# A short-convolution layer on one core: the scale's half of each later adaLN piece loaded from Pool's queue

## The chip, the core and the metric

The kernel runs on one core of a Trainium2 chip. The metric is the device time of one execution in microseconds (us). Before the change it is 904.07 us, the median of three runs (903.63 to 904.27). A profiled execution of the same kernel, whose trace is read below, took 904.01 us, of which 902.2 us are the span that the trace covers.

## The reference

With one layer, 256 tokens, a model width of 2048 and a branch width of 4096, the reference comes down to this (all in float32):

```
h = rmsnorm(x, norm_g)                              # x: 256 x 2048
mod = silu(c) @ ada_w + ada_b                       # ada_w: 2048 x 6144
shift, scale, gate = split(mod, 3)                  # 2048 each
h = h * (1 + scale) + shift
b, c_, v, g = split(h @ sc_w_in, 4)                 # sc_w_in: 2048 x 16384
u = causal_depthwise_conv(c_ * v, sc_conv_w)        # width 3
y = b * u * silu(g)
out = rmsnorm(x + gate * (y @ sc_w_out), final_g)   # sc_w_out: 4096 x 2048
```

The columns of `ada_w` lie in three blocks of 2048: those of the shift, of the scale and of the gate. No product with `sc_w_in` can be made for a row block k (128 rows of the 2048) before shift and scale of that block are known.

## The kernel before, in words

**Start.** SP issues the loads of x (four of 512 KB, L218), then the columns of `ada_w` for the first two row blocks k = 0 and 1, for shift and scale (twelve loads, 4 MB, L231), then the first weights, `raw0` (two of 256 KB, L198). VectorE (DVE) sums the columns weighted by silu(c) (L413, L415), TensorE adds them up, ScalarE (ACT) writes the high part of the modulated tokens into `hT` (L328), and Pool the low part of k = 1 (L433). All of this is pinned in the order in which it is written (`in_order`), engine by engine.

**First half of the input projection (`mm_s`).** Float32 products are made as three products of a high and a low part: a load of weights (`raw_s`, L538) is split by ACT (`hi`, L354) and DVE (`lo`, L359), and TensorE multiplies `hi` with both parts of the tokens and `lo` with the high part (L495). A function `plan()` writes down a list of steps, 16 groups of four column blocks, each taken over those row blocks that are ready by the plan's own costs, so that the groups are opened with k = 0 and 1 and finished later. What has been summed so far is kept in `acc` by ACT (L516) or DVE (L518), and put back by ACT (L528).

**adaLN behind the first group.** Between those steps the plan places 56 steps `ada`: seven groups of two row blocks, in eight pieces each. A piece (`ada_piece`) takes one of four tiles `at` (128 x 1024 floats, `bufs=4`) and fills it with two DMAs of 256 KB, one with the columns of the shift, one with those of the scale (L464), both on SP's queue. DVE adds the two halves together, with one instruction for each of the two rows in the tile (L476 for the first row of a group, L478 for all others), each over 512 columns of which 256 belong to either half. So every such instruction needs both loads. After the last piece of a group TensorE turns the sums (L485), DVE reduces them (L486), and the tokens of two more row blocks become ready (L324 to L335).

**Order on the queues.** Beyond the pinned start, the tile framework arranges each engine's queue when the kernel is built. It goes by a priority, which is the order in the program unless `later` moves it, and by which instructions have their buffers and inputs in its own model of the time. A load that needs a tile comes up for its queue when the tile's last users are done in that model. The weights have three places of 1 MB, cut in half for loads of 512 KB.

**Rest.** The second half of the input projection (`mm_b`) runs with all row blocks ready, the gate's columns are loaded into the same four tiles (`at_g`, L612) and summed over the partitions by Pool with small DMAs on its own queue (L625 and L626, their sum in L627), and then comes the output projection (L731).

Of the kernel before, what the change touches and what calls it, by code (L numbers as in the profile page):

```python
# [13 lines left out]
P = 128  # L14
# [103 lines left out]
def short_conv_layer(ctx: ExitStack, tc: tile.TileContext, x, c, norm_g, ada_w, ada_b, w_in, conv_w, w_out, final_g, out):  # L118
    nc = tc.nc
# [68 lines left out]
    @contextmanager  # L188
    def later(n):

        now = tc.cur_priority
        tc.cur_priority = now + n
        yield
        tc.cur_priority = now
# [29 lines left out]
    adas = ada_w[0].rearrange("(k p) (s f) -> p k s f", p=P, s=3)  # L224
# [229 lines left out]
    def ada_piece(k0, nk, piece):  # L454
        w = nk * P
        kk = ASLOT // (2 * w)
        if piece == 0:
            sums[k0] = adap.tile([P, 2, 2 * P], F32, tag="gv", name="gv")
        gv = sums[k0][:, :, 0:w]
        j = piece * kk  # L460
        at = adap.tile([P, ASLOT], F32, tag="at", name="at", bufs=4)
        at4 = at.rearrange("p (k s f) -> p k s f", k=kk, s=2)
        for s in range(2):
            nc.sync.dma_start(at4[:, :, s, :], adas[:, j : j + kk, s, k0 * P : k0 * P + w])  # L464
        with later(GIVE):
            ada_sums(j, kk, at4, gv)
        if j + kk == KT:
            with later(-LEAD):
                ada_done(k0, nk, gv)

    def ada_sums(j, kk, at4, gv):
        for i in range(kk):
            c_k = silu_c[:, j + i : j + i + 1]
            if j + i == 0:
                with behind(ended):
                    nc.vector.tensor_scalar_mul(gv, at4[:, i], c_k)  # L476
            else:
                nc.vector.scalar_tensor_tensor(out=gv, in0=at4[:, i], scalar=c_k, in1=gv, op0=ALU.mult, op1=ALU.add)  # L478

    def ada_done(k0, nk, gv):  # L480

        tp = psum.tile([P, 4, P], F32, tag="sm", name="tp_g", bufs=2)
        gs = const.tile([P, 4], F32, tag="gs", name="gs", bufs=2)
        for o in range(2 * nk):
            nc.tensor.transpose(tp[:, o, :], gv[:, o // nk, (o % nk) * P : (o % nk + 1) * P], ident)  # L485
        nc.vector.reduce_sum(gs[:, 0 : 2 * nk], tp[:, 0 : 2 * nk, :], axis=mybir.AxisListType.X)  # L486
        modulate(k0, nk, gs[:, 0 : 2 * nk])
# [80 lines left out]
    for kind, *step in plan():  # L568
        if kind == "ada":
            ada_piece(*step)  # L570
        else:
            ch, k1 = step[0], step[3]
            part(*step)
            if step[2] == 0 and len(acc) in LATER:
                with tc.issue_after(last_mm[0].ins), behind(ended):
                    if len(acc) == LATER[0]:
                        rows2 = rows_tile("rows2")
                        nc.sync.dma_start(rows2[:, :], conv_w.rearrange("w (k p) -> (w k) p", p=P))
                    else:
                        turn(rows2, 0, 96, cw)  # L580
            whole[ch] += k1 == KT
            if k1 == KT and whole[ch] == 4:
                mixed(ch)
# [354 lines left out]
```

## Time and profile before

| what | before |
|---|---|
| time, median of three | 904.07 us |
| profiled execution: its time, its span | 904.01 us, 902.2 us |
| TensorE busy | 887.1 us, 98% of the span |
| DVE, ACT, Pool busy | 676.2, 484.5, 88.0 us |
| first product with `sc_w_in` starts | 24.86 us |
| `mm_s` ends, `mm_b` ends | 378.56 us, 726.72 us |
| loads on the changed line (L464) | 112 of 256 KB, issued from 21.2 to 208.6 us |

Times within the trace are counted from the start of its span. In the rows of a timeline the columns are start, duration, engine, line, operation, what it writes and reads, and, in brackets, the idle time of the engine ahead of it and what ended that. SPq and POOLq are the sequencers that issue DMAs. In the table by stretches each engine's busy time is followed by the granted clock of TensorE, the mean busy share of the 16 DMA engines (it can be a little over 1, as packets overlap) and the GB/s that they moved.

### The profile page before, as it was taken

What the parts mean: (1) busy time and instruction counts of PE and PEld (TensorE: products, weight loads), DVE (VectorE), ACT (ScalarE), POOL (GpSimd) and SP (SyncE); (2) the same over time, 40 slices, a digit from 0 to 9 for tenths busy, and PEclk for the clock granted to TensorE, in tenths of its full rate; (3) what the DMA queues carried; (4) which work ended last, traced back from release to release, by engine and by line L of the source; (5) the groups of instructions that cost most, each with busy time, mean ns of one, the idle gap of its engine ahead of it and who ended that gap; (6) DMA issues with size and microseconds to landing.
All of it is one profiled execution on the core that took longest, in us unless ns stands there. A gap on an engine that the chain in (4) does not pass through costs nothing.

```text
span 902.2 us, 16405 instructions
## 1 busy us (share of the span) xinstructions
PE 887.1 (98%) x6997; PEld 850.1 (94%) x6997; DVE 676.2 (75%) x665; ACT 484.5 (54%) x429; POOL 88.0 (10%) x95
## 2 busy tenths in 40 slices
PE   7999999999999999999999999999999999999996
PEld 4899999999999999999999999999999988888885
DVE  5889989888888866765966677565555578879896
ACT  6767866665548766644433434444434445444443
POOL 0000000000000034024224203420000000000000
PEclk9999999999999999999999999999999999999999
DMA  9999999999998587688887788776666476674662
GB/s 309 367 369 369 362 313 353 351 370 354 350 328 289 162 277 245 194 257 243 282 242 241 249 283 259 232 221 199 198 188 188 141 288 224 191 275 132 197 231 94
DMA packets 159595, 235.01 MB, mean 260 GB/s; under 512 B 6805, under 2 KB 105285, under 8 KB 159137
## 3 DMA queue, kind: packets, MB, share of 16 engines
q1 hardware_dynamic: 156384, 226.56, 76.9%
q0 software_dynamic: 3008, 7.34, 2.9%
q8 instruction: 55, 0.90, 0.4%
q14 instruction: 20, 0.16, 0.0%
q10 hardware_dynamic: 128, 0.04, 0.0%
HBM read 224.49 MB, written 2.10 MB: 251 GB/s over the span
## 4 chain that ended last, share of the span: by engine, by line
PE 92%; DMA 4%; ACT 1%; SPq 1%; DVE 1%; issue 1%; ACTq 0%
PE mm_b L495 39%; PE mm_s L495 36%; PE mm_w L731 7%; PE mm_o L731 6%; PE mm L731 4%; DMA at<-in_ada_w_dram 2%; DMA raw_s<-in_sc_w_in_dram 1%; SPq L231 1%; ACT hi L354 1%; DMA raw_o<-in_sc_w_out_dram 1%; DMA x<-in_x_dram 1%; PE tp_g L485 0%; ACT mm_s L528 0%; ACT acc L516 0%; DVE lo L762 0%
## 5 line engine op out<-in xcount | busy, mean ns | idle before, releaser
L495 PE MATMUL mm_s<-hT,hi 128*128 128x256 f32 x2048 | 350.2, 277 | 1.7 <-ACT hT L328 1.0
L495 PE MATMUL mm_b<-hT,hi 128*128 128x256 f32 x2048 | 348.2, 276 | 0.0
L495 PEld LDWEIGHTS mm_s<-hT,hi 128*128 128x128 f32 x2048 | 308.4, 188 | 2.3 <-ACT hT L328 1.2
L495 PEld LDWEIGHTS mm_b<-hT,hi 128*128 128x128 f32 x2048 | 308.4, 188 | 0.0
L495 PE MATMUL mm_b<-hT,lo 128*128 128x256 f32 x1024 | 282.7, 276 | 0.0
L495 PE MATMUL mm_s<-hT,lo 128*128 128x256 f32 x1024 | 282.0, 277 | 0.1
L359 DVE TENSOR_TENSOR lo<-raw,hi 128x2048 fp32r<-128x2048 f32 (+1 forms) x66 | 151.9, 2302 | 99.6 <-ACT hi L354 99.4
L354 ACT CAST hi<-raw 128x2048 fp32r<-128x2048 f32 (+1 forms) x66 | 123.7, 1874 | 191.3 <-PE mm_b L495 152.4
L495 PEld LDWEIGHTS mm_b<-hT,lo 128*128 128x128 f32 x1024 | 192.3, 188 | 0.0
L495 PEld LDWEIGHTS mm_s<-hT,lo 128*128 128x128 f32 x1024 | 191.7, 188 | 0.3 <-DVE lo L359 0.3
L359 DVE TENSOR_TENSOR lo<-raw_s,hi 128x2048 fp32r<-128x2048 f32 (+1 forms) x80 | 149.8, 1877 | 40.5 <-ACT hi L354 39.9
L354 ACT CAST hi<-raw_s 128x2048 fp32r<-128x2048 f32 (+1 forms) x80 | 124.0, 1557 | 57.2 <-PE mm_s L495 51.2
L478 DVE SCALAR_TENSOR_TENSOR gv<-at,silu_c,gv 128x512 f32<-128x512 f32 x105 | 78.7, 749 | 3.6 <-DMA at<-in_ada_w_dram 1.9
L516 ACT COPY acc<-mm_s 128x1024 f32<-128x1024 f32 x54 | 54.7, 1014 | 42.1 <-PE mm_s L495 42.0
L359 DVE TENSOR_TENSOR lo<-raw_o,hi 128x2048 fp32r<-128x2048 f32 x22 | 50.4, 2291 | 23.4 <-ACT hi L354 23.4
L354 ACT CAST hi<-raw_o 128x2048 fp32r<-128x2048 f32 x22 | 42.0, 1908 | 46.2 <-PE mm_w L731 12.0
L627 POOL TENSOR_TENSOR gacc<-gacc,z 128x512 f32<-128x512 f32 x28 | 48.3, 1726 | 109.0 <-DMA z<-gacc 109.0
L731 PE MATMUL mm_w<-hi,y 128*128 128x512 f32 x184 | 58.8, 389 | 0.0
L731 PE MATMUL mm_o<-hi,y 128*128 128x512 f32 x176 | 55.3, 389 | 0.0
L621 DVE SCALAR_TENSOR_TENSOR gacc<-at_g,silu_c,gacc 128x512 f32<-128x512 f32 x60 | 46.9, 782 | 6.0 <-DMA at_g<-in_ada_w_dram 4.8
L625 POOL DMA_DIRECT2D z<-gacc x28 | 15.7, 560 | 348.7 <-DVE acc L562 284.7
L731 PEld LDWEIGHTS mm_w<-hi,y 128*128 128x128 f32 x184 | 34.5, 188 | 7.1
(153 smaller groups left out, 685.9 us busy)
## 6 DMA issues: line engine op xcount, KB each, us to landing
raw<-in_sc_w_in_dram SPq DMA_DIRECT2D x64, 1024.0 KB, 5.9
raw_s<-in_sc_w_in_dram SPq DMA_DIRECT2D x47, 1024.0 KB, 7.8
raw_o<-in_sc_w_out_dram SPq DMA_DIRECT2D x32, 1024.0 KB, 5.2
at<-in_ada_w_dram SPq DMA_DIRECT2D x114, 256.0 KB, 8.0
raw_s<-in_sc_w_in_dram SPq DMA_DIRECT2D x33, 512.0 KB, 7.1
at_g<-in_ada_w_dram SPq DMA_DIRECT2D x32, 512.0 KB, 7.9
at<-in_ada_w_dram SPq DMA_DIRECT2D x6, 512.0 KB, 9.4
x<-in_x_dram SPq DMA_DIRECT2D x4, 512.0 KB, 6.2
```

Of the source, the lines that this page charges most:

```text
L231: nc.sync.dma_start(at[:, :, s, :], adas[:, j : j + kk, s, 0 : NK0 * P])
L354: nc.scalar.copy(hi[:, :n], raw[:, :n])
L359: last_low[0] = nc.vector.tensor_tensor(out=lo[:, :n], in0=raw[:, :n], in1=hi[:, :n].bitcast(F32), op=ALU.subtract)
L478: nc.vector.scalar_tensor_tensor(out=gv, in0=at4[:, i], scalar=c_k, in1=gv, op0=ALU.mult, op1=ALU.add)
L495: mm = last_mm[0] = nc.tensor.matmul(dst, w, h[k], start=begins and left, stop=ends, skip_group_check=True)
L516: nc.scalar.copy(acc[ch, q], bank)
L621: nc.vector.scalar_tensor_tensor(out=ga, in0=at3[:, i, :], scalar=s, in1=ga, op0=ALU.mult, op1=ALU.add)
L625: nc.gpsimd.dma_start(turned[0 : P - away], ga[away:P])
L627: nc.gpsimd.tensor_tensor(out=ga, in0=ga, in1=turned, op=ALU.add)
L731: nc.tensor.matmul(dst, y[a], b, start=opens and i == 0, stop=ends and i == 2, skip_group_check=True)
```

## The change

Of the two DMAs of each of the 56 pieces the one with the shift's columns (s = 0) stays on SP's queue and the one with the scale's (s = 1) goes to Pool's. The tiles, the bytes, and the instructions that read them are the same.

```diff
@@ -461,7 +461,8 @@
         at = adap.tile([P, ASLOT], F32, tag="at", name="at", bufs=4)
         at4 = at.rearrange("p (k s f) -> p k s f", k=kk, s=2)
         for s in range(2):
-            nc.sync.dma_start(at4[:, :, s, :], adas[:, j : j + kk, s, k0 * P : k0 * P + w])
+            queue = (nc.sync, nc.gpsimd)[s]
+            queue.dma_start(at4[:, :, s, :], adas[:, j : j + kk, s, k0 * P : k0 * P + w])
         with later(GIVE):
             ada_sums(j, kk, at4, gv)
         if j + kk == KT:
```

The loads of the first group (L231), the weights and the gate's columns stay on SP's queue.

## The prediction, made before the changed kernel was run

> **What bounds the kernel now.** I read the page first, then the waits of TensorE in the stage that the change touches, then the table by stretches, then the chain that ended last and the timeline around the start.
>
> ```profile
> PE 887.1 (98%) x6997; PEld 850.1 (94%) x6997; DVE 676.2 (75%) x665; ACT 484.5 (54%) x429; POOL 88.0 (10%) x95
> PE mm_s L495 <- ACT hT L328: 1.0, 1, 1.0
> PE mm_s L495 <- ACT hi L354: 0.6, 1, 0.6
> ```
>
> The first row says that TensorE hardly rests. The other two are all of its waits between 24 and 110 us; from 110 to 400 us the same view shows none. So once the products with the weights have begun, at most 1.6 us can be won in the stage of the change, and each microsecond by which that beginning moves moves the end. When it begins is the first thing to look at.
>
> ```profile
> 0.00:1.00 1.00, 0.00 (x0) 0.00 (x0) 0.09 (x2) 0.00 (x0) 0.41 (x5) 1.00 0.00 0
> 1.00:2.00 1.00, 0.00 (x0) 0.00 (x0) 0.00 (x0) 0.00 (x0) 0.29 (x1) 1.00 0.32 57
> 2.00:3.00 1.00, 0.00 (x0) 0.00 (x0) 0.00 (x0) 0.87 (x1) 0.00 (x0) 1.00 0.79 143
> 3.00:4.00 1.00, 0.00 (x0) 0.00 (x0) 0.00 (x0) 0.41 (x1) 0.00 (x0) 1.00 0.85 295
> 10.00:12.00 2.00, 2.00 (x6) 0.92 (x5) 1.71 (x7) 0.03 (x1) 0.00 (x0) 1.00 1.10 363
> 18.00:20.00 2.00, 1.74 (x16) 1.74 (x17) 1.93 (x3) 2.00 (x7) 0.00 (x0) 1.00 1.10 347
> 50.00:80.00 30.00, 30.00 (x267) 30.00 (x266) 27.46 (x33) 21.18 (x20) 0.00 (x0) 1.00 1.07 370
> ```
>
> In each row the last two figures are the DMA engines' busy share and their GB/s. They are full from about 4 us on, and still full at 50 to 80 us. TensorE and DMA are both at their limit here, and DVE is at 27.46 of 30 us. These rows from the timelines of DVE, ACT and TensorE show what the start waits for:
>
> ```profile
> 13.21 0.49 DVE L413 TENSOR_SCALAR gv<-at,silu_c 128x512 f32<-128x512 f32 x1 [0.74 <-DMA at<-in_ada_w_dram]
> 16.32 6.78 DVE L415 SCALAR_TENSOR_TENSOR gv<-at,silu_c,gv 128x512 f32<-128x512 f32 x9 [0.26 <-DMA at<-in_ada_w_dram]
> 22.97 1.33 ACT L354 CAST hi<-raw 128x512 fp32r<-128x512 f32 x2 [1.84 <-DMA raw<-in_sc_w_in_dram]
> 24.86 0.74 PE L495 MATMUL mm_s<-hT,hi 128*128 128x256 f32 x4 [0.99 <-ACT hT L328]
> ```
>
> DVE starts its sums when the first columns land and is then busy without a break but for 0.26 us; ACT waits 1.84 us for `raw0`, the last load of the start. Both ways to the first product at 24.86 us begin with a DMA that waits its turn in a full queue. What lands ahead of `raw0` delays the first product.
>
> **What the change removes.** 56 issues of 256 KB each leave SP's queue (two loads of that size belong to the first group and stay).
>
> ```profile
> at<-in_ada_w_dram SPq DMA_DIRECT2D x114, 256.0 KB, 8.0
> L464 SPq DMA_DIRECT2D at<-in_ada_w_dram x112: 367/460/2052, 21.2 to 208.6; - x112
> DMA to landing us min/median/max: 4.1/8.0/9.7
> SPq L464 <- DVE gv L478: 19.5, 32, 2.2
> SPq L538 <- DVE lo L359: 146.9, 56, 8.4
> ```
>
> At a median of 0.460 us this frees 56 x 0.46 = 26 us of SP. It is worth nothing on the path: SP waits 146.9 us for weight places that DVE gives back, and 19.5 us for `at` tiles, and the half that stays on SP waits for the same tile. Without this cover the gain could be no more than the 1.6 us that TensorE waits. The bytes are unchanged: 8.0 us from issue to landing is a backlog of some 3 MB at 370 GB/s, mostly turn-taking.
>
> **What it adds to Pool.** 56 issues, on a queue whose loads the trace shows only for the gate. The first two rows are one of Pool's two issuing lines (count, then minimum, median, maximum in ns) and its time from issue to landing in us; the others are all that Pool does before 311 us, but for four constants in its first half microsecond.
>
> ```profile
> L625 POOL DMA_DIRECT2D z<-gacc x28: 532/557/698, 311.6 to 593.1; - x28
> DMA to landing us min/median/max: 2.4/3.9/8.4
> 0.74 0.20 POOL masks.py:197 MEMSET ident<- 128x128 f32 x1 [0.29 <-POOLq L925]
> 1.01 0.29 POOL masks.py:199 TENSOR_SCALAR_AFFINE_SELECT ident<-ident 128x128 f32<-128x128 f32 x1
> 26.02 0.91 POOL L433 TENSOR_TENSOR hT<-xs,hT 128x256 fp32r<-128x256 f32 x1 [24.71 <-ACT xs L429]
> ```
>
> 56 x 0.56 = 31 us of Pool, in time in which it is idle: nothing on the path. From issue to landing I expect 2.4 to 9.7 us, the ends of Pool's and of SP's rows, and take Pool's median of 3.9, since the new loads stand in no backlog of their own queue. That wins nothing either, as every sum on L478 needs the shift's half as well.
>
> **What it moves.** The order on a queue is not that of the program:
>
> ```profile
> 21.15 0.99 SPq L464 DMA_DIRECT2D at<-in_ada_w_dram  x2
> 22.19 0.47 SPq L538 DMA_DIRECT2D raw_s<-in_sc_w_in_dram  x1
> 22.70 0.98 SPq L464 DMA_DIRECT2D at<-in_ada_w_dram  x2
> 23.72 0.58 SPq L538 DMA_DIRECT2D raw_s<-in_sc_w_in_dram  x1
> 24.91 3.76 SPq L464 DMA_DIRECT2D at<-in_ada_w_dram  x4
> 30.09 0.35 SPq L578 DMA_DIRECT2D rows<-in_sc_conv_w_dram  x1
> 30.83 3.18 SPq L538 DMA_DIRECT2D raw_s<-in_sc_w_in_dram  x4
> ```
>
> In the program L578 stands behind the tenth column group, with nine loads of `raw_s` ahead of it; here it was issued after four of them. Four halves are what the free weight places hold, and eight L464 are the four pieces that the four `at` tiles hold: SP took everything that had its place, and then the far later L578, which had one too. On SP the first pieces could come no sooner than 21 us, as x and the first columns stand ahead of them. On Pool nothing does. Its first two instructions end at 1.30 us, and L433 cannot go before 26 us. So I expect the scale's halves of the first four pieces to be issued from 1.3 us on, 0.56 us each, until 3.5 us, although DVE wants them only at 28 us. Four times 256 KB are 1.05 MB; at 355 GB/s, between the rates of the two full stretches above, they hold the DMA engines for 2.95 us. Part of this fits into time in which they still idle: 0.21 us between 2 and 3 us and 0.15 between 3 and 4, 0.36 together, of which I take half, since a load that Pool issues at 1.3 us landed at the earliest 2.4 us later in the rows above. The rest, 2.8 us, is put ahead of the later loads of x, of the first columns and of `raw0`. The first product moves from 24.86 to about 27.6 us.
>
> The Trainium skill, in "DMA: Bandwidth & Descriptors", section "Queues, rings and completion order", says that each DMA engine takes turns between its queues packet by packet; this would let the early halves share the engines with x rather than wait behind it, which the rows of before cannot show.
>
> Some of it comes back. The chain of the wait at 40 us reads:
>
> ```profile
> 23.21 8.29 DMA at<-in_ada_w_dram
> 31.51 7.36 DMA raw_s<-in_sc_w_in_dram
> 38.90 1.06 ACT hi L354
> 40.00 15.80 PE mm_s L495 x137
> ```
>
> It runs through loads alone, and the bytes up to there are the same in another order; with TensorE 2.8 us later that wait of 0.64 us is gone. The other wait, of 1.0 us near 90 us, hangs on ACT's and DVE's turn at TensorE's banks, which moves with TensorE, and stays. From there on each scale's half goes out when its tile comes free, as before, and overtakes the weights in SP's backlog; never more than four tiles, so never more than another 2.95 us at once. I cost that at nothing, as DVE (27.46 of 30 us busy) and the weights now have 2.1 us more of lead; without that cover it is up to 2.95 us.
>
> The sum, against the profiled execution: 904.01 + 2.8 - 0.64 = 906.2 us. That execution lies 0.06 us below the median of 904.07, which changes nothing. The bounds of this case: at the lower end 2.95 - 0.36 with both waits recovered (1.6) is +1.0, or 905.0 us; at the upper end 2.95 with nothing recovered and half of another 2.95 in overtaken weights is +4.4, or 908.4 us.
>
> **The rivals.** First, no change. If the scale's halves go out in step with their partners, from 21 us on, the same bytes pass in the same order, and the result is 904.1 us, or down to 903.4 where the wait at 40 us shrinks. For it speaks that the engines are shared and full in any case; against it the L578 row, which shows that a free queue takes what is ready. The Trainium skill has this as its rule: in "DMA: Bandwidth & Descriptors", section "Issuing engines are not separate DMA queues", it says that DMAs issued by several engines run on the same 16 engines and that only the sequencer's issue time is saved; by that rule the 26 us of SP, which are not on the path, are all that changes. The full rows from 4 us on agree with it, but it says nothing on when a queue gets to issue.
>
> Second, clearly slower: the new loads come late, and DVE, which works in order, stands still with the splits of the weights behind it.
>
> ```profile
> 28.06 0.48 DVE L476 TENSOR_SCALAR gv<-at,silu_c 128x512 f32<-128x512 f32 x1
> 28.45 1.22 DVE L359 TENSOR_TENSOR lo<-raw_s,hi 128x1024 fp32r<-128x1024 f32 x1
> 31.62 0.75 DVE L478 SCALAR_TENSOR_TENSOR gv<-at,silu_c,gv 128x512 f32<-128x512 f32 x1 [1.29 <-DMA at<-in_ada_w_dram]
> DVE gv L478 <- DMA at<-in_ada_w_dram: 1.9, 3, 1.3
> 378.00:726.00 348.00, 348.00 (x3073) 348.00 (x3073) 221.09 (x192) 146.58 (x113) 64.66 (x67) 1.00 0.75 228
> ```
>
> The place is L476, with L359 right behind it, and TensorE behind that. If Pool's first loads were queued behind L433, they would be issued at 26.9 us and land 2.4 to 8.4 us later, at 29.3 to 35.3 us. DVE would wait 1.2 to 7.3 us, at the median of 3.9 some 2.8 us, and the later pieces, which have no lead either (the third row), could cost as much again: +2.8 to +8, so 906.8 to 912 us. It decides as soon as a half lands later than its partner's 8.0 us after a common issue. Against it stands the idle Pool queue at the start, and Pool's issue row: its maximum of 698 ns was measured in a stage of which DVE was busy for 63% (the last row), so nothing holds Pool up for long there.
>
> Third, faster: the halves are early at no cost, both waits go, and SP, freed of half of its waits for `at` tiles, gets weights out sooner: 904.0 - 1.6 = 902.4 us. To be beyond that, something in the output projection would have to move too, which the change doesn't touch.
>
> **How the numbers follow.** My forecast's case has a chance of 0.50, the rival of no change 0.25, the clearly slower one 0.17, the faster one 0.08. A difference of 0.2% or 1.8 us is about what a measurement of this kernel can tell from no change, so the border lies at 905.9 above and 902.3 below. Of the forecast's own range of 905.0 to 908.4, about a quarter by chance lies under the upper border. Slower: 0.50 x 0.74 + 0.17 = 0.54. Within: 0.13 + 0.25 = 0.38. Faster: 0.08. For eight in ten the range goes from 903.0 (the no-change case, without the faster one) to 911.0 us (most of the clearly slower one).
>
> **What would show it.** In the profile after, Pool's timeline should have four issues of L464 between 1.3 and 4 us, and the DMA rate in the first 4 us should be higher. ACT's first cast of `raw` should move from 22.97 to about 25.7 us, and TensorE's first `mm_s` from 24.86 to about 27.6; the wait of 0.6 us near 40 us should be gone, and from then on all rows of `mm_s` and `mm_b` should be the old ones moved by some 2 us. I am wrong if the first product keeps its time, if the first issues of Pool stand behind L433, or if TensorE's waits for `hi` and `lo` in 24 to 210 us grow instead of the start: then the second rival holds, and L478's waits for its loads must have grown from 1.9 us to several.

## The result, and the profile after

The changed kernel takes 908.62 us, the median of six runs (908.26 to 909.39), beside 904.04 us (903.63 to 904.53) for six runs of the kernel before: a ratio of 1.0052 with a 95% interval of 1.0041 to 1.0062. That is 4.6 us slower, where 2.1 us were forecast. The profiled execution took 908.40 us, its span is 906.6 us.

Pool's timeline after the change (start, duration, then the instruction) shows the early issues:

```profile
0.74 0.20 POOL masks.py:197 MEMSET ident<- 128x128 f32 x1 [0.29 <-POOLq L926]
1.31 0.91 POOL L465 DMA_DIRECT2D at<-in_ada_w_dram  x1 [0.37 <-issue]
2.31 0.31 POOL masks.py:199 TENSOR_SCALAR_AFFINE_SELECT ident<-ident 128x128 f32<-128x128 f32 x1
2.54 2.19 POOL L465 DMA_DIRECT2D at<-in_ada_w_dram  x3
28.57 0.90 POOL L433 TENSOR_TENSOR hT<-xs,hT 128x256 fp32r<-128x256 f32 x1 [23.84 <-ACT xs L429]
32.23 0.72 POOL L465 DMA_DIRECT2D at<-in_ada_w_dram  x1 [2.76 <-DVE gv L479]
```

Four of the scale's halves go out between 1.31 and 4.73 us, the fifth only at 32.23 us, when DVE gives a tile back. (All lines behind the edit are one higher than before: L464 is now L465, L478 is L479, L495 is L496.) What they do to the start is read from the rows that answer to those of before, DVE's, ACT's and TensorE's. The first row here is of the kernel before, the others are of the changed one:

```profile
10.29 1.23 DVE L282 SCALAR_TENSOR_TENSOR junk<-x 128x1024 f32<-128x1024 f32 x1 [0.19 <-DMA x<-in_x_dram]
12.25 1.23 DVE L282 SCALAR_TENSOR_TENSOR junk<-x 128x1024 f32<-128x1024 f32 x1 [1.55 <-DMA x<-in_x_dram]
15.73 0.48 DVE L413 TENSOR_SCALAR gv<-at,silu_c 128x512 f32<-128x512 f32 x1 [1.31 <-DMA at<-in_ada_w_dram]
25.51 1.34 ACT L354 CAST hi<-raw 128x512 fp32r<-128x512 f32 x2 [2.43 <-DMA raw<-in_sc_w_in_dram]
27.41 0.74 PE L496 MATMUL mm_s<-hT,hi 128*128 128x256 f32 x4 [1.02 <-ACT hT L328]
```

DVE's first sum stood at 13.21 us and is at 15.73; the cast of `raw0` moved from 22.97 to 25.51, the first product from 24.86 to 27.41 us. All of it is one shift of 2.52 to 2.55 us, and DVE's second square of x (L282), at 12.25 in place of 10.29 us, shows that 1.96 us of it had been lost by the time x was in.

The rest is in TensorE's waits between 24 and 110 us, and where they are is in its timeline (three rows of its waits, then three of the timeline):

```profile
PE mm_s L496 <- DVE lo L359: 1.7, 2, 1.0
PE mm_s L496 <- ACT mm_s L529: 1.2, 1, 1.2
PE mm_s L496 <- ACT hT L328: 1.0, 1, 1.0
31.33 0.39 PE L496 MATMUL mm_s<-hT,lo 128*128 128x256 f32 x1 [0.68 <-DVE lo L359]
65.78 0.38 PE L496 MATMUL mm_s<-hT,lo 128*128 128x256 f32 x1 [1.04 <-DVE lo L359]
97.57 0.50 PE L496 MATMUL mm_s<-hT,hi 128*128 128x256 f32 x2 [1.17 <-ACT mm_s L529]
```

The wait of 0.64 us near 40 us is gone. Three others are new, of 0.68, 1.04 and 1.17 us, 2.89 together. The wait of 1.0 us on L328 is in both kernels the one ahead of the first product itself, as the row at 27.41 us shows. From the first product to the end of `mm_s` TensorE needed 353.70 us before (24.86 to 378.56) and 355.79 after. Here the first row is of the kernel before:

```profile
378.56 348.16 PE mm_b L495 x3072
236.39 146.81 PE mm_s L496 x1295
383.20 348.16 PE mm_b L496 x3072
```

These are pieces of the chain that ended last, from the two input stages; `mm_b` has its 348.16 us as before. So 2.55 us are lost ahead of the first product and 2.09 behind it, 4.64 in all at the start of `mm_b`; the output projection gives 0.24 back, and the span is 4.4 us longer.

DVE's timeline has a first hint at the second loss. These are its rows around its first sum for the second group, the first one again of the kernel before:

```profile
26.91 1.22 DVE L359 TENSOR_TENSOR lo<-raw_s,hi 128x1024 fp32r<-128x1024 f32 x1 [0.59 <-ACT hi L354]
28.18 0.68 DVE L359 TENSOR_TENSOR lo<-raw,hi 128x512 fp32r<-128x512 f32 x1
29.65 0.49 DVE L477 TENSOR_SCALAR gv<-at,silu_c 128x512 f32<-128x512 f32 x1 [0.79 <-DMA at<-in_ada_w_dram]
30.06 1.22 DVE L359 TENSOR_TENSOR lo<-raw_s,hi 128x1024 fp32r<-128x1024 f32 x1
```

Before, the split of `raw_s` (L359) came first, at 26.91 us, and the sum behind it, at 28.06. Now the sum stands in front, waits 0.79 us for its load, and TensorE waits for the split at 31.33 us. The order on DVE's queue is another one, although the edit names no instruction of DVE. So the framework arranged it anew when it built the kernel; that it did so because the loads come earlier in its own model of the time is my reading, which no trace shows.

### The profile page after: what moved, and what is told of

Its sections match the earlier page's. It is cut to its first block, busy times and chain, and to the rows that moved or that the text cites. A ratio compares the mean times of both kernels' runs of the same rounds, so it can differ in the third digit from the quotient of the medians.

```text
span 906.6 us, 16460 instructions
## 1 busy us (share of the span) xinstructions
PE 888.0 (98%) x6997; PEld 850.4 (94%) x6997; DVE 673.7 (74%) x665; ACT 483.5 (53%) x429; POOL 126.1 (14%) x151
## 4 chain that ended last, share of the span: by engine, by line
PE 95%; DMA 2%; SPq 1%; ACT 1%; DVE 1%; issue 0%; ACTq 0%; DVEq 0%
PE mm_b L496 38%; PE mm_s L496 37%; PE mm_w L732 7%; PE mm_o L732 7%; PE mm L732 4%; DMA at<-in_ada_w_dram 1%; SPq L231 1%; DMA x<-in_x_dram 0%; DVE lo L359 0%; PE tp_g L486 0%; ACT hi L354 0%; ACT acc L517 0%; DVE gv L479 0%; ACT mm_s L529 0%; DVE xs L332 0%
## 5 line engine op out<-in xcount | busy, mean ns | idle before, releaser
L496 PE MATMUL mm_s<-hT,hi 128*128 128x256 f32 x2048 | 350.0, 277 | 2.2 <-ACT mm_s L529 1.2
L496 PE MATMUL mm_b<-hT,hi 128*128 128x256 f32 x2048 | 348.2, 276 | 0.0
L496 PEld LDWEIGHTS mm_s<-hT,hi 128*128 128x128 f32 x2048 | 308.4, 188 | 2.6 <-ACT mm_s L529 1.4
L496 PEld LDWEIGHTS mm_b<-hT,hi 128*128 128x128 f32 x2048 | 307.9, 188 | 0.0
L496 PE MATMUL mm_s<-hT,lo 128*128 128x256 f32 x1024 | 282.8, 277 | 1.7 <-DVE lo L359 1.7
L496 PE MATMUL mm_b<-hT,lo 128*128 128x256 f32 x1024 | 282.8, 276 | 0.0
L359 DVE TENSOR_TENSOR lo<-raw,hi 128x2048 fp32r<-128x2048 f32 (+1 forms) x66 | 152.2, 2307 | 103.6 <-ACT hi L354 103.2
L496 PEld LDWEIGHTS mm_s<-hT,lo 128*128 128x128 f32 x1024 | 191.8, 188 | 2.1 <-DVE lo L359 2.1
L496 PEld LDWEIGHTS mm_b<-hT,lo 128*128 128x128 f32 x1024 | 192.2, 188 | 0.0
L359 DVE TENSOR_TENSOR lo<-raw_s,hi 128x2048 fp32r<-128x2048 f32 (+1 forms) x80 | 148.6, 1866 | 42.7 <-ACT hi L354 42.2
L479 DVE SCALAR_TENSOR_TENSOR gv<-at,silu_c,gv 128x512 f32<-128x512 f32 x105 | 78.6, 749 | 6.1 <-DMA at<-in_ada_w_dram 4.2
L359 DVE TENSOR_TENSOR lo<-raw_o,hi 128x2048 fp32r<-128x2048 f32 x22 | 50.4, 2289 | 22.7 <-ACT hi L354 22.7
L628 POOL TENSOR_TENSOR gacc<-gacc,z 128x512 f32<-128x512 f32 x28 | 45.9, 1638 | 109.9 <-DMA z<-gacc 109.9
L465 POOL DMA_DIRECT2D at<-in_ada_w_dram x56 | 40.7, 727 | 136.0 <-DVE gv L479 127.6
```

What stands on the lines that cost most here:

```text
L359: last_low[0] = nc.vector.tensor_tensor(out=lo[:, :n], in0=raw[:, :n], in1=hi[:, :n].bitcast(F32), op=ALU.subtract)
L465: queue.dma_start(at4[:, :, s, :], adas[:, j : j + kk, s, k0 * P : k0 * P + w])
L496: mm = last_mm[0] = nc.tensor.matmul(dst, w, h[k], start=begins and left, stop=ends, skip_group_check=True)
L628: nc.gpsimd.tensor_tensor(out=ga, in0=ga, in1=turned, op=ALU.add)
```

## The experiments

Two theories stood for the second loss: the halves on Pool's queue overtake weights in the backlog, so that the splits get their data late; or the new order on the engines' queues makes the waits by itself. Each run was timed in turn with the kernel before on the same chip (904.17 us in the first four, 904.22 in the others).

**Only the later halves on Pool's queue.**

```diff
-            queue = (nc.sync, nc.gpsimd)[s]
+            queue = nc.gpsimd if s and (k0 > NK0 or piece >= 4) else nc.sync
```

> Both halves of the first four pieces are on SP's queue again, the scale's halves of the other 52 on Pool's. Theory: the change costs in two places, 2.5 us at the start (four halves ahead of the first group) and some 2.1 us in the stage behind it (halves that overtake weights, and an order of the queues made anew). Then the first product is back at 24.9 us, and what is left is the second part: 905 to 907 us. Rival, that the start is the only cause and the later waits follow from it: 904 us. Rival, that the start costs nothing by itself since the time is made up elsewhere: 908 to 909 us.

Measured: 905.23 us, ratio 1.0022 (1.0010 to 1.0033). The time is a median and the ratio is taken over all runs, here and below. The runs lie wider apart than those of any other kernel here: five at 904.47 to 905.23 us and four at 906.51 to 908.98; why is open. In the profiled one (904.79 us, of the lower five) the first product is at 24.99 us, and of the new waits none is there, but the old one near 40 us has grown from 0.64 to 1.57 us:

```profile
24.99 0.74 PE L496 MATMUL mm_s<-hT,hi 128*128 128x256 f32 x4 [0.95 <-ACT hT L328]
30.77 0.89 POOL L465 DMA_DIRECT2D at<-in_ada_w_dram  x1 [3.72 <-DVE gv L479]
34.28 0.74 POOL L465 DMA_DIRECT2D at<-in_ada_w_dram  x1 [2.62 <-DMA at<-in_ada_w_dram]
40.20 1.04 ACT L354 CAST hi<-raw_s 128x1024 fp32r<-128x1024 f32 x1 [1.03 <-DMA raw_s<-in_sc_w_in_dram]
41.29 0.51 PE L496 MATMUL mm_s<-hT,hi 128*128 128x256 f32 x2 [1.57 <-ACT hi L354]
```

SP issued the weights in question at about the same time (four from 30.61 us, from 30.83 before), two halves from Pool were issued at 30.77 and 34.28, and the cast that needs the weights stands at 40.20 us instead of 38.90. Up to 110 us the order on TensorE, DVE and ACT is, in the traces, that of the kernel before, so this wait is one for late data. It is what overtaking costs where TensorE has no lead: about 1 us, at one place, in the profiled run. What the upper four lose isn't known; by the ratio, over all runs, this kernel loses 2.0 us. The time lies in the range that I had put down, but not for the reason given there: the three new waits are not in this kernel, so they must come with the first four halves.

**Only the first four halves on Pool's queue.**

```diff
-            queue = (nc.sync, nc.gpsimd)[s]
+            queue = nc.gpsimd if s and k0 == NK0 and piece < 4 else nc.sync
```

> Only the scale's halves of the first four pieces are on Pool's queue, the other 52 on SP's. Theory: the first product at 27.4 us as in the changed kernel, one wait less near 40 us, no later waits: 905.5 to 906.5 us. Rival, that the later waits follow from the start too: 908 to 909 us. Rival, that the start is harmless: 904 us.

Measured: 908.44 us, ratio 1.0049 (1.0036 to 1.0063). My theory, that these four cost the start alone, was wrong: they bring the whole loss, the start (first product at 27.73 us) and the three later waits, at the same places:

```profile
31.65 0.38 PE L496 MATMUL mm_s<-hT,lo 128*128 128x256 f32 x1 [0.65 <-DVE lo L359]
66.10 0.39 PE L496 MATMUL mm_s<-hT,lo 128*128 128x256 f32 x1 [1.01 <-DVE lo L359]
97.87 0.50 PE L496 MATMUL mm_s<-hT,hi 128*128 128x256 f32 x2 [1.17 <-ACT mm_s L529]
```

No load of this stage goes through Pool after 5 us in this kernel, so overtaken weights cannot be their cause. What the two kernels share is the early start of four loads, and much of the order on the queues: in the traces, up to the end of `mm_s`, TensorE's differs at a single place, a transpose moved by one product, DVE's and ACT's at more of them.

**Both halves of every piece on Pool's queue.**

```diff
-            queue = (nc.sync, nc.gpsimd)[s]
+            queue = nc.gpsimd
```

> Both halves of all 56 pieces are on Pool's queue, so that twice the bytes, 2.1 MB, can go out in the first microseconds. Theory: the start's delay goes by the bytes that are put ahead: 5.1 to 5.9 us, the first product at 30 to 31 us, the time at 909 us or more (904.0 + 5.5, less a wait at 40 us, and with up to 3 us of later waits: 909 to 912). Rival, that the delay comes from the presence of a second queue and not from the bytes: the first product at 27.4 us again and 908 to 909 us.

Measured: 910.70 us, ratio 1.0073 (1.0060 to 1.0086). The time is in the range of the theory. The first product is at 31.77 us, later than the 30 to 31 us that I expected: 6.9 us later than before and more than the bytes alone would give (2.1 MB at 355 GB/s are 5.9 us). Pool issues eight loads by 7.6 us, and TensorE's clock falls behind a time in which it is short of work:

```profile
14.00:18.00 4.00, 0.85 (x6) 0.67 (x7) 0.80 (x6) 3.06 (x4) 0.00 (x0) 1.00 1.06 342
18.00:22.00 4.00, 4.00 (x24) 4.00 (x22) 2.54 (x4) 4.00 (x10) 0.00 (x0) 0.57 1.10 348
26.00:28.00 2.00, 2.00 (x11) 2.00 (x11) 1.89 (x4) 0.00 (x0) 0.00 (x0) 0.50 1.09 366
```

In this table by stretches the third figure from the right is the granted clock. TensorE was busy for 0.85 of 4 us, and in the stretch behind it had 0.57 of its clock, while it turned x; between 26 and 28 us, with half of its clock, it worked on the sums of the first group. How much of the last microsecond is the clock's was not measured by itself.

**No half ahead of L433.**

```diff
-            queue.dma_start(at4[:, :, s, :], adas[:, j : j + kk, s, k0 * P : k0 * P + w])
+            with behind(ended if s else {}):
+                queue.dma_start(at4[:, :, s, :], adas[:, j : j + kk, s, k0 * P : k0 * P + w])
```

> The scale's halves are on Pool's queue as in the changed kernel, but none may be issued ahead of the low part of k = 1 (L433), the last pinned instruction there. Theory: the first product is at 24.9 us or a little sooner, since 1 MB less stands ahead; the first four halves come at 27 us and land 3 to 9 us later, so DVE waits at the first sum for 2 to 7 us with the splits behind it, and TensorE for 1 to 5 us: 905 to 909 us. Rival, that only the early bytes cost: 904 us or less.

Measured: 915.82 us, ratio 1.0135 (1.0121 to 1.0149), the slowest of all, beyond the range that I had put down. The first product is at 24.80 us, as before; the loss is behind it, but not where I had put it. DVE does not stand still at its first sum: that sum was moved far back in its queue, behind five splits of `raw_s`, and the row blocks of the later groups were ready late (the lines stand one higher again in this kernel):

```profile
26.81 3.07 POOL L466 DMA_DIRECT2D at<-in_ada_w_dram  x4
38.56 0.48 DVE L478 TENSOR_SCALAR gv<-at,silu_c 128x512 f32<-128x512 f32 x1
PE mm_s L497 <- DVE hT L335: 4.7, 2, 3.8
PE mm_s L497 <- ACT acc L518: 2.4, 1, 2.4
```

Here, too, the order is another one; no run holds it fixed for this kernel. TensorE's waits behind the first product come to 7.4 us (4.7, 2.4 and 0.3 for `lo`) in place of 0.64, which is 6.8 us more. The clock adds to it: it was 0.83 between 80 and 90 us and 0.50 between 104 and 110, where TensorE was busy for 5.35 us. An estimate from these figures, 0.17 of 10 us and half of 5.35, is 4.4 us. Together that is 11.2 us, and this profiled execution (915.30 us) is 11.3 us longer than that of before.

**The changed kernel's loads in the order of before.** To hold the order fixed, the kernel carries the order of every instruction of TensorE, DVE, ACT and SP in the kernel before and ties each to the one in front of it on its engine, without a wait (shortened; the scale's loads that now go through Pool are not in SP's list):

```diff
+    for line in zlib.decompress(base64.b85decode(ORDER)).decode().split("|"):
+        ...
+            if front is not None:
+                tc.add_manual_dep(ins, front, after, reason="the order of the other kernel")
```

> The loads are those of the changed kernel, but TensorE, DVE, ACT and SP work through their instructions in the order of the kernel before. Theory: the 2.3 us behind the start come from the order that the framework arranged anew (DVE's first sum now stands ahead of the first split), so they go: first product at 27.4 us, no wait near 40 us, 905.5 to 906.5 us; what overtaken weights cost (1.1 us where only the later halves moved) may come on top, up to 907.2 us. Rival, that the late waits come from data that land late: 908 to 909 us as in the changed kernel.

Measured: 906.21 us, ratio 1.0022 (1.0013 to 1.0031). The start is as late as in the changed kernel, and the three later waits are gone. TensorE's timeline has this row for the first product:

```profile
27.64 0.74 PE L496 MATMUL mm_s<-hT,hi 128*128 128x256 f32 x4 [1.01 <-ACT hT L328]
```

The wait of 1.0 us in it is all that TensorE waits between 24 and 400 us. With the order held, the loads that the change moves cost 2.0 us. That 52 later halves overtake weights in this kernel costs nothing that shows: with the first four alone, in the same order, the time is 905.97 us (below). The reason may be that TensorE, which starts 2.8 us later, has the lead that it lacked in the first experiment.

**The order of the changed kernel, with all loads on SP's queue.** The same device the other way round: the order of TensorE, DVE, ACT and SP is that of the changed kernel, and each scale's half stands on SP's queue right behind its partner.

> All loads are on SP's queue, each scale's half right behind its partner, but TensorE, DVE, ACT and SP otherwise go in the order of the changed kernel. Theory: no delay of the start (first product at 24.9 us), but the later waits of 2 to 3 us for splits and for the accumulators put back: 905.5 to 907 us. Rival, that the order is harmless without the early loads: 904 us.

Measured: 906.69 us, ratio 1.0030 (1.0018 to 1.0041). No load is early, the first product is at 24.75 us, and the three waits are there again. The second row is DVE's first sum, which stands ahead of the split that TensorE waits for at 29.35 us:

```profile
24.75 0.74 PE L496 MATMUL mm_s<-hT,hi 128*128 128x256 f32 x4 [0.99 <-ACT hT L328]
27.67 0.49 DVE L477 TENSOR_SCALAR gv<-at,silu_c 128x512 f32<-128x512 f32 x1 [1.47 <-DMA at<-in_ada_w_dram]
29.35 0.39 PE L496 MATMUL mm_s<-hT,lo 128*128 128x256 f32 x1 [1.34 <-DVE lo L359]
63.83 0.39 PE L496 MATMUL mm_s<-hT,lo 128*128 128x256 f32 x1 [1.02 <-DVE lo L359]
95.62 0.50 PE L496 MATMUL mm_s<-hT,hi 128*128 128x256 f32 x2 [1.17 <-ACT mm_s L529]
```

The order alone costs 2.5 us, the loads alone 2.0; their sum of 4.5 is, within the intervals, the 4.6 us of the change. Which of the four engines' orders makes the waits (SP's is one of them) was not tested apart.

**Four and two early halves in the order of before.** The last pair asks whether the start's delay goes by the bytes that are put ahead. The edits are that of the second experiment, with `piece < 4` and `piece < 2`, and the order as above.

> Only the scale's halves of the first four pieces are on Pool's queue, and TensorE, DVE, ACT and SP go in the order of the kernel before. Theory: this is the price of the early loads alone, 2.5 to 2.9 us at the start less the wait of 0.6 us near 40 us: 905.9 to 906.5 us. Rival, that later waits come with the late start whatever the order: 908 us or more.

> As the run with four early halves in the old order, but with two. Theory: the start's delay goes by the bytes put ahead, half of them here: the first product at 26.2 to 26.4 us, the time 904.7 to 905.2 us. Rival, that it is the second queue and not the bytes: the first product at 27.4 to 27.7 us, the time as with four.

Measured: 905.97 us with four, ratio 1.0020 (1.0011 to 1.0030), and 904.77 us with two, ratio 1.0005 (0.9996 to 1.0014). The first products are at 27.49 and 25.86 us:

```profile
27.49 0.74 PE L496 MATMUL mm_s<-hT,hi 128*128 128x256 f32 x4 [1.02 <-ACT hT L328]
25.86 0.74 PE L496 MATMUL mm_s<-hT,hi 128*128 128x256 f32 x4 [0.99 <-ACT hT L328]
```

Two halves move the first product by 1.0 us, four by 2.6, eight (in the run with both halves, where the order was not held and the clock fell as well) by 6.9. So the delay grows with the bytes, and the presence of a second queue alone does not explain it. It isn't in proportion to them: at 355 GB/s two halves are 1.5 us, and the 25.86 us lie below the 26.2 to 26.4 that I expected; why is open. With four the price is near the one that was forecast for the start and its recovery (1.75 us measured, 2.1 forecast); with two it can hardly be told from nothing. No version tried here is faster than the kernel before, and none of the runs points to one.

## Why the prediction was right, and where it was not

The way and the wide range were right (903.0 to 911.0 us). The size was not: +2.1 us forecast, +4.6 measured, and 908.62 us lies just above the 908.4 at which the forecast's own case ended. It lies in the wide range only because that made room for the second rival, which did not come about; to that extent the hit was luck.

- **The early issues.** Right, four of them from 1.31 us on, ahead of L433: the queue had nothing ahead of them, and their tiles were free. Each takes Pool 0.72 us at the median, not 0.56, which costs nothing, as Pool has no other work there.
- **The start.** Right. The first product was forecast at 27.6 us and came at 27.41; 2.8 us were the term, 2.55 it measured. The part that was to fit into idle DMA time did not: the rates before and after are 57 and 33 GB/s between 1 and 2 us, 143 and 196 between 2 and 3, and 295 and 288 between 3 and 4, no more than some 20 KB in all. Why 2.55 us were lost and not the full 2.95 isn't shown. SP had issued all of x by 2.57 us and Pool one of its four loads, 0.74 us of traffic at 355 GB/s, yet x was used 1.96 us later. That bears out the turn-taking between queues that was cited from the Trainium skill, "DMA: Bandwidth & Descriptors", section "Queues, rings and completion order".
- **What comes back.** Right in size: the 0.64 us near 40 us went. The other wait was misread. The 1.0 us on L328 is not near 90 us; it is the last step to the first product at 24.86 us, whose row the prediction itself quotes with 0.99 us. Nothing in the sum hung on it, but the lower bound of 905.0 and the faster rival counted it as something to be won.
- **From there on nothing.** This is the step that failed. Behind the start I set one danger, overtaken weights, and costed it at nothing because of the lead. That reasoning held: in the order of before, the kernel with the changed loads takes 906.21 us, beside the forecast of 906.2 (that it agrees so closely is chance: the interval is about 0.8 us to either side). What was left out is that the order of the other engines' queues was not given. I had read from the L578 row that the framework issues what is ready in its model, applied this to Pool, and then took the order of every other engine from the trace of before. The new order costs 2.5 us by itself, as the run with all loads on SP's queue shows. One of the signs of being wrong was half met: the waits for `lo` in 24 to 210 us did grow, from nothing to 1.7 us, but beside the late start and not instead of it.
- **Issue to landing.** I took 3.9 us for Pool's loads, and the page of the changed kernel has a median of 6.7, within the stated bounds. SP's loads of that size have 8.8. The second rival's mark, a half that lands later than its partner, was hardly reached: taken in pairs by order of issue, Pool's half lands later in 3 of 56, by 0.7 us at most, as far as the trace tells. L479's waits for its loads in 24 to 240 us rose to 4.2 us from 1.9 all the same.
- **The rivals.** No change would need the halves in step with their partners, and the first four were not. The rule from the Trainium skill, "DMA: Bandwidth & Descriptors", section "Issuing engines are not separate DMA queues", that only issue time is saved, holds for the engines' rate, which between 50 and 80 us was 370 GB/s before and is 360 after, but not for the time: the loads issued early held up those that are waited for, by 2.55 us at the first product. The clearly slower case exists, since Pool's halves behind L433 gave 915.82 us, but with a rearranged order and a lowered clock rather than by DVE standing still at its first sum. Faster had nothing to win.

## What to carry to other kernels

Here loads put on an idle queue went out as soon as their buffers were free. Where the first compute waits for loads, count the bytes of all the buffers that are free at that moment as put ahead of it, at the full DMA rate (here 2.95 us by that count and 2.55 measured), and ask whether such loads are wanted so soon. Holding them back is no cure by itself: behind L433 it cost over 11 us, with another order on the queues. Where a framework arranges the queues, an edit to one load can rearrange engines that it does not name: compare the orders before explaining a wait by the hardware, and hold the order fixed to price the loads by themselves.

## What the runs showed of the hardware

I had not expected that TensorE's waits would bring a second price with them, its granted clock. In the kernel with both halves on Pool's queue its timeline has these two waits, the first ahead of the stretch at 0.57 that is shown above, the second ahead of the one at 0.50:

```profile
16.43 0.33 PE L311 MATMUL tp_x<-ident,x 128*128 128x128 f32 x1 [2.59 <-ACT x L386]
23.98 0.68 PE L395 MATMUL sum<-silu_c,at 128*128 128x128 f32 x4 [1.24 <-DVE gv L415]
```

The kernel with the halves behind L433 has this wait and these three stretches (the third figure from the right is the clock):

```profile
82.00 0.51 PE L497 MATMUL mm_s<-hT,hi 128*128 128x256 f32 x2 [2.43 <-ACT acc L518]
80.00:90.00 10.00, 8.00 (x56) 8.00 (x57) 9.52 (x13) 7.53 (x9) 1.78 (x3) 0.83 0.82 278
90.00:104.00 14.00, 10.82 (x96) 10.62 (x94) 10.53 (x14) 13.16 (x13) 3.27 (x5) 0.98 0.98 335
104.00:110.00 6.00, 5.35 (x25) 5.35 (x26) 5.30 (x7) 0.54 (x2) 1.05 (x2) 0.50 0.88 282
```

The clock came down in waits or right behind them: of 2.59, 2.43 and 3.8 us (the last is the longest wait on L335 above), and once, in the stretch from 26 to 28 us, with waits of no more than 1.24 and 0.74 us ahead of it. A wait of 2.10 us in the kernel with the changed loads in the order of before left it at 1.00:

```profile
15.88 0.33 PE L311 MATMUL tp_x<-ident,x 128*128 128x128 f32 x1 [2.10 <-ACT x L386]
```

The Trainium skill, in "TensorE: Matmul & The Clock Gate", section "Part 1: The HAM clock gate", describes a gate that halves the clock after an idle window of about 3.4 us and gives it back after as long a busy one. The half agrees. The length does not agree as a measure of single pauses: here the clock fell behind pauses of 2.43 and 2.59 us, and once behind shorter ones. In the profiled run of the changed kernel the clock stayed at 1.00 through the start and the stage.
